# Attention in one layer of a hybrid backbone: transposing probabilities in pairs of key tiles, and masking only the outer blocks

## Chip, core and metric

The kernel runs on one core of a Trainium2 chip, in one launch. The metric is the device time of an execution in microseconds (us). The engines are TensorE (PE, with its weight loads listed apart as PEld), VectorE (DVE), ScalarE (ACT), GpSimd (POOL) and SyncE (SP), which issues the DMAs. TensorE writes only to PSUM, which has 8 banks of 512 fp32 values per partition; ScalarE and VectorE read the results from there.

## What is computed

One layer over 1024 latent tokens of width 1024, with a prefix of 256 context tokens. The part that the change touches is the two attention branches. Each has 8 query heads and 2 key/value heads of width 64. The local one sees the 256 context keys, the query block of 128 and its two neighbours, and a sink term in the softmax; the global one sees all 256 + 1024 keys.

```python
def window_attn(q, k, v, ck, cv, sink):            # local
    ...
    valid = (jnp.abs(kpos - qpos) <= WINDOW) & (kpos >= 0) & (kpos < S)   # WINDOW = BLOCK = 128
    s_loc = jnp.where(valid, s_loc, NEG_BIG)
    ...
    p = jax.nn.softmax(jnp.concatenate([s_ctx, s_loc, s_sink], axis=-1), axis=-1).astype(v.dtype)
    o = (jnp.einsum('bkgnqj,bjkd->bnqkgd', p[..., :n_ctx], cv)
         + jnp.einsum('bkgnqj,bnjkd->bnqkgd', p[..., n_ctx:n_ctx + 3 * BLOCK], vb))

def dense_attn(q, k, v, sink=None):                # global, in blocks of 128 queries
    s = jnp.einsum('bqkgd,bjkd->bkgqj', q.reshape(B_, Lq, KV, G, hd), k).astype(jnp.float32) * hd ** -0.5
    p = jax.nn.softmax(s, axis=-1)[..., :k.shape[1]].astype(v.dtype)
    return jnp.einsum('bkgqj,bjkd->bqkgd', p, v).reshape(B_, Lq, HQ * hd)
```

A key at most 128 positions away is valid. So in the middle block all 128 x 128 pairs are valid, in the block before it the keys from the query's own place on, and in the block after it the keys up to that place.

## The kernel before

**The whole.** The kernel goes through its stages one after the other: modulation and norms, projections of the context and of the latent tokens, the recurrence, token-major projections with rotary factors, local attention, global attention, the merge of the branches, and the gated MLP. Matrix products are done in fp32r, a rounded fp32 type: an operand is split into a rounded high part and the rest as a low part (on ScalarE and VectorE), and two or three products are summed.

**Order of the work.** The kernel is written for a framework that tracks the data, sets the semaphores and plans the order of each engine's instructions when it is built. The order of the program is the priority; `tc.high_priority(offset=...)` raises it. A planner then takes the first instruction that it holds to be ready, so that an engine's order can differ from the program's. On the chip each engine works in its planned order. `weave` (L1214) mixes generators in the program's order: it advances the one that has done the smallest share of its steps, by the number of steps given beside it.

**Attention.** `attention` (L1229) runs once for each branch (`br` 0 local, 1 global). Its loop has 16 iterations `it`: 8 query tiles `tt` of 128 queries by 2 key/value groups `g` of 4 heads. In each, three generators are woven: `scores(it + 1)`, `values(it)`, and gate products of another projection as filler (`gz`, L199 to L201). `qprep(it + 2)` loads and transposes queries ahead (`pq`, L1286). A query is held as high and low halves in one 128-row operand, so that a product with KH and one with KL gives the full score.

**Local scores** (`softmax_window`, L1374). For each head: two products of 256 columns with the context keys (L1387, L1388), two with the local keys (L1390, L1391), of 384 columns, or 256 at the first and last query tile, and one product of the identity with a table of 0 and -1e30 (`trir`, three blocks of 128 columns: before, middle, after) over all the local columns, which adds the mask (L1392). The middle block of the table is all zero. The maximum is taken on VectorE (L1395), the exponential on ScalarE (L1399), and GpSimd divides by the sum (L1409).

**Global scores** (`softmax_global`, L1415). There is no mask; the maximum is taken at L1427 and L1439, the exponentials at L1442 and L1443, and the division follows after the product with the values (`pr` L1316, `Rs` L1318).

**Values** (`values`, L1299). There are 10 key tiles in the global branch, 5 in the local one (4 at its two ends). For each key tile: four transposes of the heads' probabilities by the identity into one PSUM bank `pp` (L1321), a rounded copy `ph` on ScalarE (L1325), the rest `pl = pp - ph` on VectorE (L1326), and, two tiles later (`PV_LAG`), two products with the values, which sum in `po` (L1307, L1308). `pp`, `pq` and `pr` share two PSUM banks (tag "a"); `po` and the gate products share two others (tag "b"); the scores have the remaining four. `ph` and `pl` have three buffers each. Then `po` is put together on ScalarE and VectorE and stored (L1334 to L1344).

Of the kernel before, what the change touches and what calls it, by code (L numbers as in the profile page):

```python
# [9 lines left out]
F32 = mybir.dt.float32  # L10
F32R = mybir.dt.float32r
U32 = mybir.dt.uint32
AF = mybir.ActivationFunctionType
ALU = mybir.AluOpType
# [4 lines left out]
P = 128  # L19
# [41 lines left out]
PV_BUF = 3  # L61
PV_LAG = 2
V_PRIO = 15
# [1150 lines left out]
def weave(*gens):  # L1214

    gens = [[g, max(n, 1), 0] for g, n in gens if g is not None]
    while gens:
        gens.sort(key=lambda e: e[2] / e[1])
        e = gens[0]
        try:  # L1220
            next(e[0])
            e[2] += 1
            if e[2] > 4 * e[1]:
                raise RuntimeError("step count")
        except StopIteration:
            gens.remove(e)


def attention(tc, nc, ap_, br, ins, kv_d, q_d, y_d, mm2, bank, ident, identr, fill_gen, fill_steps):  # L1229
    V, A, G, T, SP = nc.vector, nc.scalar, nc.gpsimd, nc.tensor, nc.sync  # L1230

    def tl(shape, tag, nm, bufs=2, dt=F32):
        return ap_.tile(shape, dt, tag=tag, name=f"{tag}{br}_{nm}", bufs=bufs)

    NK = 10
    KH = tl([P, 2, NK * P], "KH", 0, 1, F32R)
    KL = tl([P, 2, NK * P], "KL", 0, 1, F32R)
    VHL = tl([P, NK, 2, 2, 64], "VHL", 0, 1, F32R)
    if br == 0:
        tri = tl([P, 3 * P], "tri", 0, 1, F32)  # L1240
        SP.dma_start(tri, ins["tri"])
        trir = tl([P, 3 * P], "trir", 0, 1, F32R)
        A.copy(trir, tri)
        snk = tl([P, 8], "snk", 0, 1)
        SP.dma_start(snk, ins["sink"].to_broadcast([P, 8]))
        nsnk = tl([P, 8], "nsnk", 0, 1)
        V.tensor_scalar(out=nsnk, in0=snk, scalar1=-1.0, scalar2=None, op0=ALU.mult)

    def prep(k0):
        kv = tl([P, 2, 256], "qf", f"kv{k0}")  # L1250
        SP.dma_start(kv, kv_d[k0:k0 + 2].rearrange("k p n -> p k n"))
        kx = kv[:, :, :128].rearrange("p k (g e) -> p k g e", g=2)
        vx = kv[:, :, 128:].rearrange("p k (g e) -> p k g e", g=2)
        vh, vl = VHL[:, k0:k0 + 2, :, 0], VHL[:, k0:k0 + 2, :, 1]
        A.copy(vh, vx)
        V.tensor_tensor(out=vl, in0=vx, in1=vh.bitcast(F32), op=ALU.subtract)
        for part, dst in ((0, KH), (1, KL)):
            if part == 0:
                kk = tl([P, 2, 2, 2, 64], "qs", f"kk{k0}{part}", dt=F32R)
                A.copy(kk[:, :, :, 0], kx)  # L1260
                A.copy(kk[:, :, :, 1], kx)
                kh = kk
            else:
                kk = tl([P, 2, 2, 2, 64], "qs", f"kk{k0}{part}", dt=F32R)
                for dup in range(2):
                    V.tensor_tensor(out=kk[:, :, :, dup], in0=kx, in1=kh[:, :, :, 0].bitcast(F32), op=ALU.subtract)
            pt = bank("a", f"kt{br}{k0}{part}", (P, 2, 2, P), F32R)
            for k in range(2):
                for g in range(2):
                    T.transpose(pt[:, g, k], kk[:, k, g].rearrange("p a b -> p (a b)"), identr)  # L1270
            A.copy(dst[:, :, k0 * P:(k0 + 2) * P].rearrange("p g (k c) -> p g k c", k=2), pt)

    QTs = {}

    def qprep(it):

        tt, g = divmod(it, 2)
        qf = tl([P, 4, 64], "qf", f"q{it}")
        SP.dma_start(qf, q_d[tt][:, g * 256:(g + 1) * 256])
        qs = tl([P, 4, 2, 64], "qs", f"q{it}", dt=F32R)  # L1280
        A.activation(qs[:, :, 0], qf, AF.Copy, scale=QSCALE)
        V.scalar_tensor_tensor(out=qs[:, :, 1], in0=qf, scalar=QSCALE, in1=qs[:, :, 0].bitcast(F32),
                               op0=ALU.mult, op1=ALU.subtract)
        pq = bank("a", f"pq{br}{it}", (P, 4, P), F32R)
        for h in range(4):
            T.transpose(pq[:, h], qs[:, h].rearrange("p a b -> p (a b)"), identr)  # L1286
        QT = tl([P, 4, P], "QT", it, 3, F32R)
        A.copy(QT, pq)
        QTs[it] = QT

    def scores(it):
        tt, g = divmod(it, 2)
        QT = QTs.pop(it)
        if br == 0:
            yield from softmax_window(nc, tl, mm2, tt, g, f"{it}_", QT, KH, KL, trir, identr, snk, nsnk, res)
        else:
            yield from softmax_global(nc, tl, mm2, g, f"{it}_", QT, KH, KL, res, rs)

    def values(it, PT, kts):  # L1299
        tt, g = divmod(it, 2)  # L1300
        Rs = None
        po = bank("b", f"po{br}{it}", (P, 4, P))
        prev = []

        def pv(n, kt, ph, pl):
            vv = VHL[:, kt, g].rearrange("p a b -> p (a b)")
            T.matmul(po, vv, ph, start=n == 0, stop=False)  # L1307
            T.matmul(po, vv, pl, start=False, stop=n == len(kts) - 1)  # L1308

        for n, kt in enumerate(kts):  # L1310
            if it in rs and n == 2:

                r = rs.pop(it)
                pr = bank("a", f"pr{br}{it}", (P, 2, P))
                for a in range(2):
                    T.matmul(pr[:, a], r[:, a * P:(a + 1) * P], ident, start=True, stop=True)  # L1316
                Rs = tl([P, 2, P], "ytmp", f"R{it}")
                A.copy(Rs, pr)  # L1318
            pp = bank("a", f"pp{br}{it}{kt}")
            for h in range(4):  # L1320
                T.transpose(pp[:, h], PT(h, n), ident)  # L1321
            ph = tl([P, 4, P], "ph", f"{it}{kt}", PV_BUF, F32R)
            pl = tl([P, 4, P], "pl", f"{it}{kt}", PV_BUF, F32R)
            with tc.high_priority(offset=V_PRIO):
                A.copy(ph, pp)  # L1325
                V.tensor_tensor(out=pl, in0=pp, in1=ph.bitcast(F32), op=ALU.subtract)  # L1326
            prev.append((n, kt, ph, pl))
            if len(prev) > PV_LAG:
                pv(*prev.pop(0))
            yield  # L1330
        for e in prev:
            pv(*e)

        yT = tl([P, 2, P], "yT", it)  # L1334
        pv_ = po.rearrange("p (a r) c -> p a r c", r=2)
        tmp = tl([P, 2, P], "ytmp", it)
        A.copy(tmp[0:64], pv_[64:128, :, 0])
        A.copy(tmp[64:128], pv_[0:64, :, 1])
        for r in range(2):
            sl = slice(r * 64, r * 64 + 64)  # L1340
            V.tensor_tensor(out=yT[sl], in0=pv_[sl, :, r], in1=tmp[sl], op=ALU.add)
        if Rs is not None:
            V.tensor_tensor(out=yT, in0=yT, in1=Rs, op=ALU.mult)
        SP.dma_start(y_d[br].rearrange("k p t -> p k t")[:, 2 * g:2 * g + 2, tt * P:(tt + 1) * P], yT)  # L1344
        yield

    n_it = 2 * LT
    res, rs = {}, {}
    def lead():
        for k0 in range(0, NK, 2):  # L1350
            prep(k0)
            yield
        qprep(0)
        qprep(1)
        yield
        yield from scores(0)

    weave((lead(), 10 + br), (some(fill_gen, FILL0), FILL0))
    fill_steps -= FILL0
    man = ExitStack()  # L1360
    if MAN[br]:
        man.enter_context(tc.manual_schedule(engines={mybir.EngineType.PE}))
    for it in range(n_it):
        PT, kts = res.pop(it)
        if it + 2 < n_it:
            qprep(it + 2)
        a, b = (min(fill_steps, int(fill_steps * i / (n_it - SKEW[br]))) for i in (it, it + 1))
        weave((scores(it + 1), S_LEN * (4 + br)) if it + 1 < n_it else (None, 0),
              (values(it, PT, kts), len(kts) + 1),
              (some(fill_gen, b - a), b - a))  # L1370
    man.close()


def softmax_window(nc, tl, mm2, tt, g, nm, QT, KH, KL, trir, identr, snk, nsnk, res):  # L1374
    V, A, G, T = nc.vector, nc.scalar, nc.gpsimd, nc.tensor
    lo, hi = max(tt - 1, 0), min(tt + 1, LT - 1)
    kts = [0, 1] + [2 + b for b in range(lo, hi + 1)]
    nk = len(kts) * P
    w = nk - 256
    m0 = (lo - (tt - 1)) * P  # L1380
    Ps = []
    st = tl([P, 8, 4], "st", nm)
    ng, sm, sk = st[:, 0], st[:, 1], st[:, 2]
    for h in range(4):

        sc = mm2(f"sa{nm}{h}").rearrange("p a b -> p (a b)")[:, 256:256 + nk]
        T.matmul(sc[:, :256], QT[:, h], KH[:, g, :256], start=True, stop=False)  # L1387
        T.matmul(sc[:, :256], QT[:, h], KL[:, g, :256], start=False, stop=True)  # L1388
        k = (2 + lo) * P
        T.matmul(sc[:, 256:], QT[:, h], KH[:, g, k:k + w], start=True, stop=False)  # L1390
        T.matmul(sc[:, 256:], QT[:, h], KL[:, g, k:k + w], start=False, stop=False)  # L1391
        T.matmul(sc[:, 256:], identr, trir[:, m0:m0 + w], start=False, stop=True)  # L1392
        n1 = ng[:, h:h + 1]
        hs = g * 4 + h
        V.tensor_reduce(out=n1, in_=sc, axis=AX.X, op=ALU.max, negate=True)  # L1395
# [5 lines left out]
        if h % NB == NB - 1:  # L1401
            b = slice(h - NB + 1, h + 1)
# [174 lines left out]
```

## Time and profile before

| what | value |
|---|---|
| median of 3 runs | 2129.76 us (2128.22 to 2130.08) |
| the profiled execution, its own time | 2129.82 us |
| its span in the trace | 2127.9 us |
| local attention, about | 700 to 885 us |
| global attention, about | 910 to 1220 us |
| transposes of probabilities (L1321) | 236 groups of four |
| rounded copies (L1325), mean | 236, 587 ns |
| subtractions (L1326), mean | 236, 687 ns |

The profile comes from one execution. Its page lists the busy time of each engine, the chain of waits that ended last, and groups of instructions by line and tile; `out<-in` names the tile written and those read. A matmul's bar in it reaches from its start to a modelled end, so that bars of consecutive matmuls overlap; starts are recorded. A busy TensorE is therefore not a TensorE without gaps. Other views of the trace list the waits of each engine, the busy time in a given stretch, and the instructions in order of time.

### The profile page before, as it was taken

To read this page: it belongs to the slowest core of one execution; us is meant where nothing else is said; L and a number is where in the kernel's file an instruction comes from. 1 tells how busy PE (TensorE), PEld (TensorE's weight loads), DVE (VectorE), ACT (ScalarE), POOL (GpSimd) and SP (SyncE) were. 2 spreads that over 40 slices of the span, in tenths; PEclk is the share of its full clock that TensorE was granted. 3 is DMA by queue.
4 is the path that set the end of the run, shared out by engine and by line. 5 is a ranking of instruction groups with operands and counts; after the bars stand their busy time and mean duration, and the time that the engine had idled before them with its cause. 6 is when DMAs were issued, how large, how long until landed. Compare 5 with 4: busy or idle time off the path is not lost.

```text
span 2127.9 us, 30555 instructions
## 1 busy us (share of the span) xinstructions
PE 2085.8 (98%) x11686; PEld 1743.1 (82%) x11686; DVE 1380.5 (65%) x2299; ACT 1001.2 (47%) x1761; POOL 288.1 (14%) x257
## 2 busy tenths in 40 slices
PE   7999999999999999999999999999999999999997
PEld 4888888888988888878888788888888888888887
DVE  4736756636665777678887746569777777664423
ACT  4333333311123777678888734346445544453222
POOL 0000000010021222100000000011333344100111
PEclk9999999999999999999999999999999999999999
DMA  9511111136543211211100354641222222285342
GB/s 359 207 44 36 46 50 41 46 113 214 186 137 123 78 59 41 80 55 35 35 28 28 115 200 142 194 156 55 99 79 89 80 80 88 81 287 201 109 126 86
DMA packets 95490, 229.28 MB, mean 108 GB/s; under 512 B 10736, under 2 KB 35824, under 8 KB 94320
## 3 DMA queue, kind: packets, MB, share of 16 engines
q1 hardware_dynamic: 95344, 227.33, 32.1%
q8 instruction: 92, 1.51, 0.3%
q14 instruction: 54, 0.44, 0.1%
HBM read 181.68 MB, written 45.61 MB: 107 GB/s over the span
## 4 chain that ended last, share of the span: by engine, by line
PE 69%; DVE 3%; ACT 2%; issue 1%; DMA 1%; POOL 1%; SPq 0%; DVEq 0%; ACTq 0%; POOLq 0%
PE pp L1321 4%; PE gz L199 3%; PE dn L929 3%; PE dn L928 3%; PE dn L930 3%; PE gz L200 3%; PE gz L201 3%; PE up L852 2%; PE up L853 2%; PE up L854 2%; PE po L1307 2%; PE po L1308 2%; PE br L200 2%; PE br L201 2%; PE br L199 2%; PE upd L853 2%
## 5 line engine op out<-in xcount | busy, mean ns | idle before, releaser
L175 ACT CAST wh<-wr 128x1024 fp32r<-128x1024 f32 (+1 forms) x139 | 145.1, 1044 | 398.7 <-PE dn L929 69.1
L176 DVE TENSOR_TENSOR wl<-wr,wh 128x1024 fp32r<-128x1024 f32 (+1 forms) x139 | 171.1, 1232 | 221.1 <-ACT wh L175 206.7
L1326 DVE TENSOR_TENSOR pl<-pp,ph 128x512 fp32r<-128x512 f32 x236 | 159.3, 687 | 29.2 <-ACT ph L1325 23.5
L199 PE MATMUL gz<-hh,wh 128*128 128x512 f32 x384 | 156.3, 408 | 3.1 <-ACT gs L523 3.1
L1325 ACT CAST ph<-pp 128x512 fp32r<-128x512 f32 x236 | 135.7, 587 | 37.4 <-PE pp L1321 35.3
L201 PE MATMUL gz<-hh,wl 128*128 128x512 f32 x384 | 152.3, 397 | 0.0
L200 PE MATMUL gz<-hl,wh 128*128 128x512 f32 x384 | 152.1, 396 | 0.0
L210 PE MATMUL tm<-wl,hh 128*128 128x256 f32 x384 | 108.9, 283 | 3.3 <-DVE wl L176 3.3
L209 PE MATMUL tm<-wh,hh 128*128 128x256 f32 x384 | 108.9, 284 | 0.9 <-ACT qo L615 0.9
L211 PE MATMUL tm<-wh,hl 128*128 128x256 f32 x384 | 108.6, 283 | 0.0
L1307 PE MATMUL po<-ph,VHL 128*128 128x512 f32 x236 | 106.1, 450 | 1.4 <-ACT ph L1325 1.0
L929 PE MATMUL dn<-ac,wh 128*128 128x512 f32 x256 | 99.7, 390 | 0.0
L930 PE MATMUL dn<-ac,wl 128*128 128x512 f32 x256 | 99.6, 389 | 0.0
L928 PE MATMUL dn<-ac,wh 128*128 128x512 f32 x256 | 99.6, 390 | 0.0
L1308 PE MATMUL po<-pl,VHL 128*128 128x512 f32 x236 | 97.1, 411 | 0.1
L199 PEld LDWEIGHTS gz<-hh,wh 128*128 128x128 f32 x384 | 72.7, 189 | 17.2 <-ACT gs L523 5.2
L201 PEld LDWEIGHTS gz<-hh,wl 128*128 128x128 f32 x384 | 72.5, 189 | 15.0
L200 PEld LDWEIGHTS gz<-hl,wh 128*128 128x128 f32 x384 | 72.8, 190 | 11.6
L210 PEld LDWEIGHTS tm<-wl,hh 128*128 128x128 f32 x384 | 73.7, 192 | 4.3 <-DVE wl L176 4.0
L1321 PE MATMUL pp<-ident,plat 128*128 128x128 f32 x512 | 76.6, 273 | 0.0
L1321 PEld LDWEIGHTS pp<-ident,plat 128*128 128x128 f32 x512 | 62.7, 140 | 16.9 <-DVE pl L1326 1.2
L199 PE MATMUL br<-yh,wh 128*128 128x512 f32 x192 | 74.3, 390 | 1.6 <-ACT yh L1468 1.6
(1420 smaller groups left out, 5898.7 us busy)
## 6 DMA issues: line engine op xcount, KB each, us to landing
wr<-in_w_cm SPq DMA_DIRECT2D x48, 512.0 KB, 3.7
wr<-in_w_up SPq DMA_DIRECT2D x44, 512.0 KB, 3.5
wr<-in_w_down SPq DMA_DIRECT2D x33, 512.0 KB, 3.5
wmr<-in_w_mod SPq DMA_DIRECT2D x32, 512.0 KB, 4.5
gate_d<-gs SPq DMA_DIRECT2D x48, 256.0 KB, 2.3
sgt<-gate_d SPq DMA_DIRECT2D x24, 512.0 KB, 3.4
act_d<-u SPq DMA_DIRECT2D x22, 512.0 KB, 2.6
st<-act_d SPq DMA_DIRECT2D x44, 256.0 KB, 4.5
```

Source lines behind the costliest of these rows:

```text
L175: A.copy(hi[:, :n], raw[:, :n])
L176: (lo_eng or V).tensor_tensor(out=lo[:, :n], in0=raw[:, :n], in1=hi[:, :n].bitcast(F32), op=ALU.subtract)
L199: T.matmul(psl, wh[:, k, c], hh[:, k0 + k, cols], start=s, stop=False)
L200: T.matmul(psl, wh[:, k, c], hl[:, k0 + k, cols], start=False, stop=False)
L201: T.matmul(psl, wl[:, k, c], hh[:, k0 + k, cols], start=False, stop=e)
L210: T.matmul(psl, hh[:, k, toks], wl[:, k % 4, :], start=False, stop=False)
L928: T.matmul(z, w[0][:, c], h[0], start=s, stop=False)
L929: T.matmul(z, w[0][:, c], h[1], start=False, stop=False)
L930: T.matmul(z, w[1][:, c], h[0], start=False, stop=e)
L1307: T.matmul(po, vv, ph, start=n == 0, stop=False)
L1321: T.transpose(pp[:, h], PT(h, n), ident)
L1326: V.tensor_tensor(out=pl, in0=pp, in1=ph.bitcast(F32), op=ALU.subtract)
```

## The change

**Values.** Key tiles are taken in pairs. The transposes of both tiles are issued first, into both banks; then, for each tile of the pair, the products of the oldest waiting tile if two are waiting, and the copy and the subtraction of this tile. With an odd number of tiles the last is alone. The place of `pr` stays ahead of the third tile. A step of the generator is a pair now, and the number of steps given to `weave` follows: 6 instead of 11 in the global branch, 4 or 3 instead of 6 or 5 in the local one.

**Mask.** The product with the mask is made for each outer block by itself (128 columns), not for the middle one, and it is issued between the two products with the local keys. A middle query tile has two such products for each head, the first and the last query tile one.

```diff
-        for n, kt in enumerate(kts):
-            if it in rs and n == 2:
+        def cast(n, kt, pp):
+            ph = tl([P, 4, P], "ph", f"{it}{kt}", PV_BUF, F32R)
+            pl = tl([P, 4, P], "pl", f"{it}{kt}", PV_BUF, F32R)
+            with tc.high_priority(offset=V_PRIO):
+                A.copy(ph, pp)
+                V.tensor_tensor(out=pl, in0=pp, in1=ph.bitcast(F32), op=ALU.subtract)
+            prev.append((n, kt, ph, pl))
+
+        for n0 in range(0, len(kts), 2):
+            if it in rs and n0 == 2:
...
-            pp = bank("a", f"pp{br}{it}{kt}")
-            for h in range(4):
-                T.transpose(pp[:, h], PT(h, n), ident)
-            ph = tl([P, 4, P], "ph", f"{it}{kt}", PV_BUF, F32R)
-            pl = tl([P, 4, P], "pl", f"{it}{kt}", PV_BUF, F32R)
-            with tc.high_priority(offset=V_PRIO):
-                A.copy(ph, pp)
-                V.tensor_tensor(out=pl, in0=pp, in1=ph.bitcast(F32), op=ALU.subtract)
-            prev.append((n, kt, ph, pl))
-            if len(prev) > PV_LAG:
-                pv(*prev.pop(0))
+            pps = []
+            for n in range(n0, min(n0 + 2, len(kts))):
+                pp = bank("a", f"pp{br}{it}{kts[n]}")
+                for h in range(4):
+                    T.transpose(pp[:, h], PT(h, n), ident)
+                pps.append((n, kts[n], pp))
+            for e in pps:
+                if len(prev) == 2:
+                    pv(*prev.pop(0))
+                cast(*e)
             yield
...
-              (values(it, PT, kts), len(kts) + 1),
+              (values(it, PT, kts), (len(kts) + 1) // 2 + 1),
...
-        T.matmul(sc[:, 256:], QT[:, h], KL[:, g, k:k + w], start=False, stop=False)
-        T.matmul(sc[:, 256:], identr, trir[:, m0:m0 + w], start=False, stop=True)
+        for b in range(lo, hi + 1):
+            if b != tt:
+                o = 256 + (b - lo) * P
+                T.matmul(sc[:, o:o + P], identr, trir[:, (b - tt + 1) * P:(b - tt + 2) * P], start=False, stop=False)
+        T.matmul(sc[:, 256:], QT[:, h], KL[:, g, k:k + w], start=False, stop=True)
```

More of the change, by code (lines that the diff above doesn't have):

```diff
@@ L1379, in softmax_window @@
     w = nk - 256
-    m0 = (lo - (tt - 1)) * P
     Ps = []
```

## The prediction, made before the change was run

> **What bounds the kernel now.** I read the page's totals first, then the busy time of the two attention stages by themselves, then TensorE's waits inside them, and last the timeline around the lines that change.
>
> ```profile
> span 2127.9 us, 30555 instructions
> PE 2085.8 (98%) x11686; PEld 1743.1 (82%) x11686; DVE 1380.5 (65%) x2299; ACT 1001.2 (47%) x1761; POOL 288.1 (14%) x257
> ```
>
> ```profile
> 700.00:885.00 185.00, 182.23 (x1086) 156.40 (x1085) 145.59 (x445) 135.64 (x345) 49.63 (x64) 1.00 0.17 51
> 910.00:1220.00 310.00, 303.92 (x1742) 247.66 (x1741) 246.24 (x406) 253.53 (x534) 6.43 (x16) 1.00 0.14 46
> ```
>
> The first pair of rows is the page's, the second the busy time by stretch: length, then TensorE, its weight loads, VectorE, ScalarE, GpSimd, and after them the granted clock. The stretch from 700 to 885 us is the local attention, 910 to 1220 us the global one; all of the edit lies in these 495 us. TensorE is busy for 98% of both at full clock. VectorE and ScalarE stand at 73 to 82%: not the bound, but with little room when work comes in bursts. So in these stages a microsecond of TensorE work more or less is nearly a microsecond of time, and beside it only TensorE's waits can give or take.
>
> Its waits show better on the weight loads than on the matmuls, since a matmul's bar includes the time in which it drains, and short gaps vanish under it. These are the rows, for 700 to 1220 us, of the operations that the pairing reorders (waited for, total, times, longest):
>
> ```profile
> PEld po L1307 <- ACT ph L1325: 6.0, 19, 1.0
> PEld pr L1316 <- issue: 5.4, 11, 1.2
> PEld pp L1321 <- ACT QT L1288: 3.6, 10, 0.5
> PEld pp L1321 <- DVE pl L1326: 1.4, 5, 0.4
> PEld pp L1321 <- issue: 1.2, 5, 0.4
> PEld pp L1321 <- POOL pw L1409: 1.1, 4, 0.3
> PEld po L1308 <- DVE pl L1326: 1.0, 4, 0.5
> PEld pp L1321 <- ACT ytmp_R L1318: 1.0, 4, 0.2
> ```
>
> Together 20.7 us: the most that another order of transposes and products could win. The wait that pairing might make worse, a transpose that waits for the subtraction to free its PSUM bank (pp <- pl), is 1.4 us today.
>
> **The mask, step by step.** Before, every head and query tile has one mask product (L1392); after, one product of 128 columns for each outer block.
>
> ```profile
> L1392 PEld LDWEIGHTS sa<-trir,identr x64: 187/188/192, 700.0 to 876.9; 128*128 128x128 f32 x64
> L1392 PE MATMUL sa<-trir,identr x64: 277/336/343, 700.1 to 877.1; 128*128 128x384 f32 x48, 128*128 128x256 f32 x16
> ```
>
> That is 48 products of 384 columns (query tiles 1 to 6) and 16 of 256 columns (tiles 0 and 7). After, the 48 become 96 and the 16 stay 16, all of 128 columns: 112 products, 48 more than now, for 14,336 columns instead of 22,528. Whether that is a gain hangs on what a product of 128 columns costs. A bar's length doesn't tell (it has the drain in it); the distance from one start to the next does. The timeline of TensorE in the local attention (start, length):
>
> ```profile
> 760.32 0.28 PE L1387 MATMUL sa<-KH,QT 128*128 128x256 f32 x1
> 760.43 0.28 PE L1388 MATMUL sa<-KL,QT 128*128 128x256 f32 x1
> 760.55 0.34 PE L1390 MATMUL sa<-KH,QT 128*128 128x384 f32 x1
> 760.73 0.34 PE L1391 MATMUL sa<-KL,QT 128*128 128x384 f32 x1
> 760.90 0.33 PE L1392 MATMUL sa<-trir,identr 128*128 128x384 f32 x1
> 761.07 0.39 PE L199 MATMUL gz<-hh,wh 128*128 128x512 f32 x1
> ...
> 761.77 0.60 PE L1321 MATMUL pp<-ident,pw 128*128 128x128 f32 x4
> 762.12 0.48 PE L1307 MATMUL po<-ph,VHL 128*128 128x512 f32 x1
> 762.44 0.39 PE L1308 MATMUL po<-pl,VHL 128*128 128x512 f32 x1
> 762.67 0.40 PE L199 MATMUL gz<-hh,wh 128*128 128x512 f32 x1
> ```
>
> From 760.55 to 760.73 to 760.90 to 761.07 a product of 384 columns costs 0.175 us; from 760.32 to 760.55 one of 256 costs 0.115 us, and the mask's 16 of that size are put at the same. The masks of before thus cost 48 x 0.175 + 16 x 0.115 = 10.2 us. No masking product of 128 columns exists in this trace. The nearest row is the last projection (L928 to L930), which has 128 columns, operands of the same rounded type, and a new weight load for each:
>
> ```profile
> 2110.62 0.28 PE L930 MATMUL dl<-ac,wl 128*128 128x128 f32 x1
> 2110.74 0.28 PE L928 MATMUL dl<-ac,wh 128*128 128x128 f32 x1
> 2110.85 0.28 PE L929 MATMUL dl<-ac,wh 128*128 128x128 f32 x1
> 2110.96 0.28 PE L930 MATMUL dl<-ac,wl 128*128 128x128 f32 x1
> ```
>
> Three distances make 0.34 us, 0.113 each: as much as 256 columns. So there seems to be a floor of some 0.11 us for a product with its own weight load, and the new masks have such a load each. 112 x 0.113 = 12.7 us, against 10.2: **2.5 us more**. Per head in the middle, two products at 0.226 replace one at 0.175, +0.051 us; at the edges the price is unchanged. The other end is a price by columns, a third of 0.175, or 0.058: 112 x 0.058 = 6.5 us, 3.7 us less than before. I take the floor, because the row that shows it is of the same kind in columns, type and loads; -3.7 stays as the other end. The Trainium skill speaks for this other end: "TensorE: Matmul & The Clock Gate", section "Back-to-back issue gap", gives N / 2.4 + 2.5 ns for a warm isolated matmul, about 56 ns at 128 columns, by which the masks would fall to an estimated 6.3 us. The projection's rows at the full clock are twice that, so the measurement decides.
>
> The mask moves ahead of the last QK product; the head's maximum (L1395) still waits for one last product, 0.05 us later than now. Other products on TensorE hide that, as its 98% shows; without that cover the 48 heads would add 2.4 us once more.
>
> **The pairing.** It adds and removes no instruction and no transfer: 944 transposes, 236 casts, 236 subtractions and 472 products remain, and every DMA keeps its place on SP's queue. What moves, in program order, is T(n) P(n-2) T(n+1) P(n-1) to T(n) T(n+1) P(n-2) P(n-1), with casts behind the products that are two tiles older. Does an alternation between transposes and products cost something that halving it would save? The first product after transposes has a bar of 0.48 us where the others have 0.39. But the starts say otherwise: from 761.77 to 762.44 four transposes and one product take 0.67 us, and 762.44 to 762.67 is 0.23 for a product alone, so 0.44, or 0.11 each, is left for the transposes. That is the same floor again; the long bar only begins early, under the last transpose. I count a gain of **0**. The misreading would be worth 118 alternations x 0.09 = 10.6 us, which I don't believe.
>
> What is late next? The second transposes of a pair need the bank that the second subtraction of the pair before frees. The global attention has 16 x 10 key tiles in 310 us, 1.94 us each or 3.88 for a pair. The planner there has already put two groups of transposes close together once, with everything that frees their banks:
>
> ```profile
> 1061.01 1.12 ACT L1442 ACTIVATE plat<-sbl,st__10486 128x1024 f32<-128x1024 f32 x1
> ...
> 1061.24 0.60 PE L1321 MATMUL pp<-ident,plat 128*128 128x128 f32 x4
> ...
> 1062.11 0.50 ACT L1443 ACTIVATE pc__10487<-pc__10487,st__10486 128x256 f32<-128x256 f32 x1
> 1062.14 0.60 PE L1321 MATMUL pp<-ident,plat 128*128 128x128 f32 x4
> ...
> 1062.61 1.06 ACT L1325 CAST ph<-pp 128x512 fp32r<-128x512 f32 x2
> ...
> 1063.21 1.29 DVE L1326 TENSOR_TENSOR pl<-pp,ph 128x512 fp32r<-128x512 f32 x2 [0.36 <-ACT ph L1325]
> ```
>
> Although ScalarE was held by an exponential, both banks were free at 1063.21 + 1.29 = 1064.50, 3.26 us after the first transpose. The next pair's second group comes on average 3.88 + 0.44 = 4.32 us after it: 1.06 us to spare. So the typical pair costs nothing, and that cover, not any gain, is what I count on; if ScalarE or VectorE come over 1.06 us later than here, the rest is a stall. For the waits listed above I take no net change, with 3 us either way.
>
> **The sum.** The profiled execution took 2129.82 us (span 2127.9 and 1.9 around it), 0.06 above the median of 2129.76, so nothing needs correcting. 2129.8 + 2.5 + 0 = **2132.3 us**, 0.12% more; about 0.2% (4.3 us) is what a measurement of this kernel can tell from no change. Own range of this case: 2128 to 2136.
>
> **Rivals.**
>
> *The banks become the bound (slower).* TensorE takes products in order, so a transpose that waits for a bank holds up its pair's products, the next scores and the gate products behind it. One subtraction (half of the 1.29 us, 0.65) is what the mate adds to the release. There are 80 full pairs in the global and 32 in the local attention; if one pair in eight waits that long, 14 x 0.65 = 9.1 us: 2129.8 + 2.5 + 9.1 = 2141.4. It decides from the third such pair on, where 4.3 is passed. For it: VectorE and ScalarE at 80%, and only two banks. Against it: the planner fills a transposer's wait with gate or score products where it foresees one, and today's pp <- pl is 1.4 us. The Trainium skill, same page, section "Part 2: What happens when you issue a matmul", says that only weight loads are pulled ahead and matmuls stay in program order; the wait rows, which sit on weight loads, do not contradict it. Chance 0.22.
>
> *The waits shrink (faster).* Products two tiles older now stand behind eight transposes instead of four, so their cast is surer to be done (6.0 and 1.0 us of waits), and the casts of one tile overlap the subtraction of the other. If half of the 20.7 us goes, 2129.8 + 2.5 - 10.3 = 2122.0. Against it: pr and QT, 9.0 us of the sum, wait for things that pairing doesn't touch. Chance 0.18.
>
> *The mask is paid by columns.* 2129.8 - 3.7 = 2126.1, within 0.2%. For it only proportion speaks; against it the projection's 0.113. Chance 0.08.
>
> *The pairing isn't executed*, because the planner pulls the groups apart again. Then only the mask is left, and the time is the forecast's; it is part of that case.
>
> **How the numbers follow.** Forecast 0.52, with 0.43 of it within 0.2%, 0.08 above (2134.1 and more) and 0.01 below; the column price 0.07 same and 0.01 faster. Faster: 0.18 + 0.01 + 0.01 = 0.20; same 0.50; slower: 0.22 + 0.08 = 0.30. For eight in ten, the range goes from 2123 (most of the shrinking waits) to 2140 (most of the bank case).
>
> **What would show it.** Right: 112 masking products whose starts lie 0.11 us apart, about 12.7 us of them; a product after transposes still with a 0.48 us bar, in half as many places; pp <- pl below some 4 us; the listed waits within 3 us of 20.7 in sum. Wrong: masking products 0.06 us apart (column price); pp <- pl or pp <- ph among the largest waits (bank case); po <- ph and pr fallen by half (the faster case); or a difference that lies outside the two attention stages, of which nothing above speaks.

## The result and the profile after

The changed kernel takes 2141.65 us (median of 4 runs, 2137.59 to 2142.64) against 2129.92 us: a ratio of 1.0057, 95% interval 1.0045 to 1.0069. It is 11.7 us slower, and the prediction's range (2123 to 2140) does not hold it. The profiled execution of after is the fastest of its four, 2137.59 us, so its trace shows 7.8 of the 11.7 us.

The totals of after's page:

```profile
span 2135.8 us, 30641 instructions
PE 2089.4 (98%) x11734; PEld 1747.6 (82%) x11734; DVE 1386.2 (65%) x2299; ACT 1000.9 (47%) x1761; POOL 290.3 (14%) x257
```

TensorE has the 48 products more that the change adds and is "98% busy" as before; this view shows nothing of what happened. Where the time went is told by the first starts of three lines, which mark the beginning of the local attention, of the global one, and of the merge. Before (the numbers behind the durations are the first and the last start):

```profile
L1387 PE MATMUL sa<-KH,QT x64: 274/281/384, 699.6 to 876.6; 128*128 128x256 f32 x64
...
L1425 PE MATMUL sbc__8873<-KH,QT x4: 278/280/282, 909.1 to 910.3; 128*128 128x256 f32 x4
...
L199 PE MATMUL br<-yh,wh x192: 389/389/498, 1204.6 to 1344.7; 128*128 128x512 f32 x192
```

After:

```profile
L1394 PE MATMUL sa<-KH,QT x64: 274/280/387, 696.8 to 887.4; 128*128 128x256 f32 x64
...
L1436 PE MATMUL sbc__8921<-KH,QT x4: 280/282/283, 920.1 to 921.3; 128*128 128x256 f32 x4
...
L199 PE MATMUL br<-yh,wh x192: 387/389/506, 1212.0 to 1352.1; 128*128 128x512 f32 x192
```

The local attention takes 223.3 us instead of 209.5, 13.8 more. The global one takes 291.9 instead of 295.5, 3.6 less. What lies ahead of them is 2.8 us shorter and what follows 0.5 us longer, though no line of it was changed; so a difference of some 3 us between two traces needn't come from the change.

The waits on TensorE's weight loads from 700 to 1220 us, after, with the same operations as in the prediction:

```profile
PEld pp L1332 <- POOL pw L1420: 12.5, 19, 1.1
PEld po L1307 <- ACT ph L1314: 4.7, 14, 1.2
PEld pr L1325 <- issue: 4.6, 14, 0.5
PEld po L1308 <- DVE pl L1315: 4.4, 10, 0.5
PEld pp L1332 <- DVE pl L1315: 3.1, 7, 1.2
PEld pp L1332 <- ACT QT L1288: 1.9, 5, 0.5
PEld pp L1332 <- issue: 1.7, 5, 0.4
...
PEld pp L1332 <- ACT ytmp_R L1327: 0.5, 2, 0.2
```

One row stands out: transposes that wait for `pw`, the probabilities which GpSimd has divided by their sum, rose from 1.1 to 12.5 us. Only the local branch has this step. The wait for PSUM banks (pp <- pl) rose from 1.4 to 3.1. The eight rows add up to 33.4 us, where the prediction's eight make 20.7.

The timeline shows how this wait arises. After, around the end of one local iteration, TensorE first:

```profile
762.02 0.33 PE L1402 MATMUL sa<-trir,identr 128*128 128x128 f32 x2
762.19 0.39 PE L1403 MATMUL sa<-KL,QT 128*128 128x384 f32 x1
762.42 0.39 PE L199 MATMUL gz<-hh,wh 128*128 128x512 f32 x1
```

```profile
765.32 0.34 PE L1397 MATMUL sa<-KH,QT 128*128 128x384 f32 x1
765.49 0.33 PE L1402 MATMUL sa<-trir,identr 128*128 128x128 f32 x2
765.66 0.39 PE L1403 MATMUL sa<-KL,QT 128*128 128x384 f32 x1
765.89 1.37 PE L1332 MATMUL pp<-ident,pw 128*128 128x128 f32 x8
767.02 0.48 PE L199 MATMUL gz<-hh,wh 128*128 128x512 f32 x1
```

then the last head's maximum, exponential and division on the three other engines:

```profile
762.98 0.82 DVE L1406 TENSOR_REDUCE st__6928<-sa 128x1 f32<-128x640 f32 x1
```

```profile
764.08 0.79 ACT L1410 ACTIVATE pw<-sa,st__6928 128x640 f32<-128x640 f32 x1 [1.22 <-DVE st__6928 L1408]
```

```profile
765.64 0.80 POOL L1420 TENSOR_SCALAR pw<-pw,st__6928 128x640 f32<-128x640 f32 x1 [0.78 <-DVE st__6928 L1418]
```

The product behind the last head's starts at 762.42; the head's division ends at 765.64 + 0.80 = 766.44, 4.0 us later. TensorE's other work until the next iteration's transposes lasts until 765.89, 3.5 us. So the fourth transpose, the last head's, waits: the eight transposes would take 8 x 0.109 = 0.87 us, and they take 1.13, from 765.89 to 767.02. In the same place before, the last head's products were done at 761.07 (its row is in the prediction) and the transposes came at

```profile
765.41 0.60 PE L1321 MATMUL pp<-ident,pw 128*128 128x128 f32 x4
```

4.3 us later: the last tile's transposes and two products with the values stood between, which after stand ahead of the last head. A busy share of 98% cannot show this; the 12.5 us, spread over 16 iterations, are waits of at most 1.1 us.

The mask's price can be read here as well. From 765.49 to 765.89 the two masks and the last product take 0.40 us, where the last product and the one mask took 2 x 0.175 = 0.35 us before: 0.05 more, as predicted. But the starts don't lie 0.11 us apart. In the 32 middle heads that a gate product follows, the medians are 0.060 us from the first mask to the second, 0.109 from the second to the last product, and 0.229 from that to the gate product, where a product of 384 columns had 0.175. The price shows in the sum alone; the first distance by itself looks like the price by columns.

### The profile page after: what moved, and what is told of

Same layout as the page of the kernel before. It is cut to its first block, busy times and chain, and to the rows that moved or that the text cites. A ratio compares the mean times of both kernels' runs of the same rounds, so it can differ in the third digit from the quotient of the medians.

```text
span 2135.8 us, 30641 instructions
## 1 busy us (share of the span) xinstructions
PE 2089.4 (98%) x11734; PEld 1747.6 (82%) x11734; DVE 1386.2 (65%) x2299; ACT 1000.9 (47%) x1761; POOL 290.3 (14%) x257
## 4 chain that ended last, share of the span: by engine, by line
PE 64%; DVE 5%; ACT 3%; issue 2%; DMA 2%; POOL 1%; SPq 0%; ACTq 0%; POOLq 0%; DVEq 0%
PE pp L1332 4%; PE dn L929 3%; PE dn L930 3%; PE dn L928 3%; PE up L852 2%; PE up L853 2%; PE up L854 2%; PE gz L199 2%; PE gz L201 2%; PE gz L200 2%; PE po L1307 2%; PE br L200 2%; PE br L199 2%; PE br L201 2%; PE po L1308 2%
## 5 line engine op out<-in xcount | busy, mean ns | idle before, releaser
L1307 PE MATMUL po<-ph,VHL 128*128 128x512 f32 x236 | 101.1, 429 | 1.5 <-ACT ph L1314 1.0
L733 ACT ACTIVATE u<-c,cw 128x1024 f32<-128x1024 f32 x38 | 47.3, 1246 | 61.7 <-DVE c L889 33.2
L200 PE MATMUL br<-yl,wh 128*128 128x512 f32 x192 | 75.0, 392 | 0.3 <-DVE yl L1480 0.3
```

The source lines that it names most:

```text
L200: T.matmul(psl, wh[:, k, c], hl[:, k0 + k, cols], start=False, stop=False)
```

## The experiments

The theory formed from this: **the steps**. `weave` advances the values of one iteration by pairs now, so the last head of the next iteration's scores enters the program after all transposes, and GpSimd's result comes late. Rivals: **the banks** (a pair waits for the subtraction of the pair before), and **the mask** beyond its price. Each run is compared with the kernel before on the same chip, where that had medians of 2125.7 to 2128.7 us; ratios carry 95% intervals, and 0.1% is 2.1 us. Beside the time stands at places the length of the local attention in the run's trace, from the first score product to the first of the global attention (209.5 us before, 223.3 after); it comes from one execution each.

### The two halves

`e1_mask`: the diff of L1390 to L1392 alone.

> The mask alone, with the values stage of before. All theories price the mask at +0.047 us in each of 48 middle heads, 2.3 us: 2132.2 us against 2129.9, from 2131 to 2134. If the earlier place of the mask (between the two products with the local keys) upsets the planned order, the time is 2135 or more and the transposes' wait for GpSimd (pp <- pw, 12.5 us after and 1.1 before) is above 6 us.

Ratio 1.0030 (1.0019 to 1.0041), 6.4 us, with 216.0 us of local attention. More than the price of the products.

`e2_pair`: the rest of the diff alone.

> The pairing alone, in both branches, with the mask of before. If the loss comes from the pairing, whether by its steps or by its banks, 2139.4 us (the 2141.65 of after without 2.3), from 2136 to 2141, and pp <- pw stays at 9 us or more. If mask and pairing only hurt together, 2131 or less.

Ratio 1.0022 (1.0014 to 1.0031), 4.7 us, with 213.8 us of local attention and pp <- pw at 7.4. The expected 9.5 missed because the mask has the larger half. The two add up to 11.1, near the whole. Their waits on the weight loads (690 to 1230 us), with the mask alone:

```profile
PEld po L1308 <- DVE pl L1326: 5.9, 15, 0.5
...
PEld pp L1321 <- POOL pw L1412: 4.4, 7, 0.8
PEld sa L1386 <- ACT pw L1402: 2.6, 7, 0.7
```

and with the pairing alone:

```profile
PEld pp L1332 <- POOL pw L1417: 7.4, 14, 0.9
...
PEld pp L1332 <- DVE pl L1315: 4.8, 15, 1.2
```

### Where the pairing loses

`e3_pair_global`: pairs in the global branch alone. The diff of its pairs is against the changed kernel; the mask is that of before.

```diff
-        for n0 in range(0, len(kts), 2):
+        W = 2 if br == 1 else 1
+        for n0 in range(0, len(kts), W):
...
-              (values(it, PT, kts), (len(kts) + 1) // 2 + 1),
+              (values(it, PT, kts), (len(kts) + 1) // 2 + 1 if br == 1 else len(kts) + 1),
```

> Pairing in the global branch alone, mask and local branch as before. Theory of the steps (the local branch loses, because the next iteration's last scores come too late for GpSimd): the global stage is 3.6 us shorter as in the profile after, so 2126.3 us, from 2124.5 to 2129. Theory of the banks (each pair waits for the subtraction of the pair before): the 80 global pairs pay most of it, 2134 or more, and pp <- pl is above 6 us.

Ratio 0.9998 (0.9990 to 1.0007): no loss, which is against the banks, and no gain that can be told from zero; pp <- pl is 4.0 us. The local attention, unchanged here, takes 208.7 us. The 3.6 us that after's profile seemed to win in the global stage are not in the time.

`e4_steps`: no pairs, only the coarser steps.

```diff
-            yield
+            if n % 2 or n == len(kts) - 1:
+                yield
...
-              (values(it, PT, kts), len(kts) + 1),
+              (values(it, PT, kts), (len(kts) + 1) // 2 + 1),
```

> No pairing and the mask of before: transposes and products alternate by single tiles as before, but a step of the generator covers two tiles, and weave is given the smaller number of steps. Theory of the steps: the last head's scores are issued late again, so pp <- pw is 8 us or more and the time 2135 to 2141 us. Theory of the banks: nothing waits that did not wait before, 2129.9 us, within 2 us.

Ratio 1.0019 (1.0011 to 1.0027), as much as the pairing alone though below the 5 us and more that the theory asked for; the local attention takes 213.5 us, and the wait is there although transposes and products alternate by single tiles:

```profile
PEld pp L1321 <- POOL pw L1410: 8.5, 14, 1.0
```

`e13_pair_tile_steps` is the counterpart: pairs, the mask of before, a step for each tile and the old number of steps.

```diff
                 pps.append((n, kts[n], pp))
+                if n == n0 and n0 + 1 < len(kts):
+                    yield
...
-              (values(it, PT, kts), (len(kts) + 1) // 2 + 1),
+              (values(it, PT, kts), len(kts) + 1),
```

> Pairing with the mask of before, but the generator gives way after each tile and weave has the old number of steps. If the pairing's 4.7 us come from the coarser steps alone, the time is that of before within 1.5 us and pp <- pw is about 1 us; if some of it belongs to products that wait for both tiles, +2 to +3 us; if all of it, +4.7.

Ratio 1.0007 (0.9997 to 1.0017), 1.5 us, with 210.7 us of local attention and pp <- pw back at its value of before:

```profile
PEld pp L1332 <- POOL pw L1419: 1.1, 4, 0.3
```

Together the two runs show that the coarser steps carry most of the pairing's loss; what is left for the pairs themselves can't be told from zero.

`e8_pair_early` and `e5_early` keep the coarse steps and move the scores ahead.

```diff
-        weave((scores(it + 1), S_LEN * (4 + br)) if it + 1 < n_it else (None, 0),
+        weave((scores(it + 1), S_LEN * 5 if br else 10) if it + 1 < n_it else (None, 0),
```

> Pairing alone as in the run with pairing and the mask of before (4.7 us slower than before), and weave is told that the local scores have 10 steps instead of 5.4, so that the last head's scores enter the program's order earlier against the coarser values steps. Theory of the steps: pp <- pw falls from 7.4 to 2 us or less, and the time comes back to that of before, from -2 to +2 us. Theory of the pairs themselves (eight transposes in a row need a bank or an operand too early, in whatever order): still +4 us or more.

Ratio 1.0019 (1.0010 to 1.0028): the wait for GpSimd goes as expected, and the time stays. The rows of 690 to 930 us show what took its place:

```profile
PEld sa L1395 <- ACT pw L1407: 5.6, 16, 0.5
PEld gz L199 <- ACT gs L523: 4.0, 10, 0.8
PEld po L1308 <- DVE pl L1315: 3.4, 13, 0.5
...
PEld pp L1332 <- POOL pw L1417: 1.5, 5, 0.5
```

There is PSUM space for the scores of two heads. Where a head now follows closely on the one before, as at 755.26 us with one other product between, it waits until the exponential of the head two before it has read that space, and starts 0.14 us after its end. So removing the wait for GpSimd alone doesn't bring the time back. With coarse steps, the heads either come late or crowd: that the steps cost the time is shown, that they do it through this one wait is not.

> The whole change, with the local scores earlier in the same way (10 steps instead of 5.4). Theory of the steps: the pairing's 4.7 us go and the mask's 6.4 us stay, +5 to +8 us against before, pp <- pw below 6 us. If the mask's products and the late scores wait for the same thing (GpSimd's chain after the last head), both go: +2.3 us for the mask's products alone, from +1 to +4. If order has nothing to do with it: +10 or more.

With the mask of the change: 1.0039 (1.0025 to 1.0052), 8.3 us; sa <- pw is 9.2 us, pp <- pw 1.4. Its median is below that of the whole change, but the intervals overlap, and neither half is gone.

`e7_tile_steps`: the whole change with a step for each tile.

> The whole change, but the generator gives way after the first tile of a pair as well, and weave is given the old number of steps. Theory of the steps: as for the whole change with earlier scores, +5 to +8 us. Theory of the pairs: +10 us or more, since the products still come after both tiles.

Ratio 1.0041 (1.0028 to 1.0054), 8.7 us, between what the two theories said; pp <- pw is 1.1 us, and po <- pl 5.1, as with the mask alone.

### Where the mask loses

From the start of a middle head's first product to the start of the gate product behind it, the traces give 0.764 us before and 0.812 with the mask alone (medians): 48 x 0.048 = 2.3 us. That leaves 4 of the 6.4.

`e9_mask_place`: the old mask, between the two products.

```diff
-        T.matmul(sc[:, 256:], QT[:, h], KL[:, g, k:k + w], start=False, stop=False)
-        T.matmul(sc[:, 256:], identr, trir[:, m0:m0 + w], start=False, stop=True)
+        T.matmul(sc[:, 256:], identr, trir[:, m0:m0 + w], start=False, stop=False)
+        T.matmul(sc[:, 256:], QT[:, h], KL[:, g, k:k + w], start=False, stop=True)
```

> Neither pairs nor blocks: the one masking product of before over all local columns, moved between the two products with the local keys. If the mask's loss beyond its 2.3 us (6.4 measured with the mask alone) comes from the place, +4 us here, with po <- pl and pp <- pw grown as there; if it comes from the number and size of the products, no change, within 1 us.

Ratio 0.9995 (0.9986 to 1.0004), with 208.5 us of local attention. Not the place.

`e10_mask_end`: the blocks, behind the last product.

> Masking products of 128 columns on the outer blocks, as in the change, but behind the last product with the local keys, where the one mask of before stands; values as before. If the loss of the mask alone (6.4 us, of which 2.3 are the products' own price) hangs on the blocks, +5 to +8 us again; if it takes the blocks and the place together, +2.3 us, from +1 to +4.

Ratio 1.0021 (1.0013 to 1.0030), 4.5 us, just below what was expected, with 216.1 us of local attention; from 690 to 930 us po <- pl is 5.5 and pp <- pw 3.7 us, where the mask alone has 5.3 and 4.4. It hangs on the blocks.

`e11_mask_256`: two products of 256 columns.

```diff
-        T.matmul(sc[:, 256:], identr, trir[:, m0:m0 + w], start=False, stop=True)
+        for o in range(0, w - 128, 128):
+            T.matmul(sc[:, 256 + o:512 + o], identr, trir[:, m0 + o:m0 + o + 256], start=False, stop=o + 256 == w)
```

> The mask as two products of 256 columns in the middle query tiles (both cover the middle block, where the table is zero), one of 256 at the edges; place and values as before. TensorE pays 2 x 0.118 instead of 0.175 us in 48 heads, +2.9 us, a little more than with blocks of 128. If the rest of the mask's loss comes because TensorE has a product more in every head, +6 us or more; if it comes because products of 128 columns are planned otherwise than they run, only +2.9 us, from +2 to +4.

Ratio 1.0012 (1.0004 to 1.0021), 2.6 us: about the price, 48 x 0.061 = 2.9 us, though TensorE pays no less than with the blocks; a middle head takes 0.825 us. On the same chip the blocks at the same place cost 3.3 us more. In the trace the local attention takes 213.8 us, 4.3 more than before, so that some 1.5 us beyond the price are not excluded. The waits of 690 to 930 us keep the shape of before:

```profile
PEld po L1307 <- ACT ph L1325: 3.6, 11, 1.0
PEld pq L1286 <- DVE qs_q L1282: 2.5, 4, 0.9
...
PEld pp L1321 <- POOL pw L1410: 1.1, 4, 0.3
```

`e12_mask_one`: one block of 128 for each head; it leaves out the mask of the block after the query's own in the middle tiles.

```diff
-        T.matmul(sc[:, 256:], QT[:, h], KL[:, g, k:k + w], start=False, stop=False)
-        T.matmul(sc[:, 256:], identr, trir[:, m0:m0 + w], start=False, stop=True)
+        b = lo if lo < tt else hi
+        o = 256 + (b - lo) * P
+        T.matmul(sc[:, o:o + P], identr, trir[:, (b - tt + 1) * P:(b - tt + 2) * P], start=False, stop=False)
+        T.matmul(sc[:, 256:], QT[:, h], KL[:, g, k:k + w], start=False, stop=True)
```

> One masking product of 128 columns for each head, in the place of the change; values as before. It leaves out the mask of the block after the query's own in the middle tiles. 64 products at 0.112 us are 7.2 us against 10.3, 3.1 us less on TensorE. If the loss follows TensorE's time, this is 3 to 5 us faster than before; if a product of 128 columns upsets the planned order whatever it costs, -3.1 + 4.1 = +1 us, from 0 to +3.

Ratio 1.0008 (0.9999 to 1.0016), with 210.3 us of local attention. A middle head falls to 0.703 us, so TensorE does save its 3 us, and the kernel is not faster. The saving reappears as waits:

```profile
PEld po L1307 <- ACT ph L1325: 5.1, 11, 1.0
PEld gz L199 <- ACT gs L523: 1.8, 6, 0.8
PEld sa L1387 <- ACT pw L1401: 1.6, 3, 0.8
```

against 1.8, 1.0 and 0.5 us before, in the same stretch. This fits two readings: products of 128 columns are planned otherwise than they run, or the other engines' chains hold this stage. Four runs with TensorE's order in the local branch taken from the program were to tell them apart:

```diff
-MAN = (False, False)
+MAN = (True, False)
```

> Before, but TensorE's order in the local attention is that of the program, written by weave, instead of the planner's. It is the base for the next three. The planner hides waits, so this may be slower than before by up to 10 us; all theories agree on it.

Ratio 1.0056 (1.0043 to 1.0070), 2138.76 us: a fixed order is 12 us slower, with 220.9 us of local attention and a long wait for GpSimd:

```profile
PEld pp L1321 <- POOL pw L1409: 9.6, 6, 2.0
```

Part of it is the clock. In the traces of all four runs with the fixed order TensorE is granted half the clock for 3.4 us at about 708 us, inside the local attention, and in this one a second time at 820.6 us; the trace of before has no such stretch there. Each can cost at most 1.7 us.

> The mask of the change (blocks of 128 columns between the two products), TensorE's order in the local attention that of the program, so that the products keep their places among the others. If the 4 us beyond the products' price come from the planner's other order, this is 2.3 us above the base with the fixed order, from 1 to 4. If the chip itself pays them around a product of 128 columns, 6 us or more above it.

1.0073 (1.0060 to 1.0086), 2141.87 us: 3.1 us above the fixed base in the medians, near the price of 2.3. But intervals of 0.13% each way can't part 2.3 from 6. The traces lean to the price: 222.4 us of local attention against 220.9, 1.5 more, or at most 3.2 if the base's second half-clock stretch cost its full 1.7.

> One masking product of 128 columns for each head and the fixed order; it leaves out the mask of the block after the query's own in the middle tiles. TensorE pays 3.1 us less than the base with the fixed order. If TensorE's time is returned in full, -3.1 us, from -4.5 to -1.5; if the local stage is held by the other engines' chains, so that less work on TensorE is only more waiting, 0, from -1 to +1.

1.0060 (1.0045 to 1.0076), 2140.96 us: 3.1 us less on TensorE, and the median is not below the base's. But the six runs go from 2134.5 to 2142.7 us, and the intervals leave room for the 3.1 us; this run decides nothing by itself. The wait of the scores for the exponential (sa <- pw) grows from 1.9 to 4.9 us.

> Pairing alone with the mask of before and the fixed order in the local attention. Theory of the steps: the program's order itself issues the last head too late, so against the base with the fixed order the loss is as large as with the planner or larger, +4 us or more, with pp <- pw among the largest waits. If the planner made the loss, 0, within 1.5 us.

1.0023 (1.0013 to 1.0033), 2131.10 us: against both theories, pairing with a fixed order is 7.7 us faster than the fixed base, of which the base's second half-clock stretch is at most 1.7. Its wait for GpSimd is about half of the base's:

```profile
PEld pp L1332 <- POOL pw L1417: 5.0, 11, 0.9
```

So pairs with coarse steps are not bad in themselves; they are worse than the order which the planner makes of the fine steps, and better than the fine steps in the program's order.

The traces of the mask's runs also show what the planner did. The table takes the instructions of the local attention in the order of their starts, by the tiles that they write and read, and counts the places where they differ from before: of TensorE's 1152 products and transposes without the masks, and of VectorE's 466 instructions. It counts the tiles, of 76, whose subtraction `pl` starts more than 0.4 us after the copy `ph` has ended, and gives the wait po <- pl from 690 to 930 us.

| mask | TensorE, other places | VectorE, other places | late subtractions | po <- pl, us |
|---|---|---|---|---|
| before | | | 14 | 0.4 |
| one of 384 columns, between the products | 0 | 0 | 14 | 0.4 |
| two of 256 columns | 19 | 94 | 15 | 0.2 |
| one block for each head | 58 | 115 | 17 | 0.6 |
| blocks, at the end | 97 | 181 | 29 | 5.5 |
| blocks, in the place of the change | 105 | 176 | 29 | 5.3 |

So the planner does order the work of both engines otherwise for the blocks, and VectorE's subtractions come late with it. The runs with a fixed order left VectorE's order to the planner: with the blocks 30 subtractions are late there, without them 20, and po <- pl is 5.1 us against 1.3. They test TensorE's share of the planner's order, then, and not VectorE's.

## Why the prediction was wrong

**The price of the mask's products was right.** 0.051 us a head were predicted and 0.048 measured, 2.3 us instead of 2.5. In sum the floor of 0.11 us for a product of 128 columns holds; by columns a head would have taken about 0.705 us and not 0.812. But the sign named for it, starts 0.11 us apart, did not come: they are 0.060 and 0.109, with the rest on the product behind, and by the prediction's own sign 0.06 would have meant the price by columns. The 56 ns of the Trainium skill's formula for an isolated matmul ("TensorE: Matmul & The Clock Gate", section "Back-to-back issue gap") are near that first distance, but half of the price.

**No cost for alternating was right.** The global branch, with 80 pairs, gained nothing (0.9998), where the misreading's 0.09 us for each pair would have been 7.2 us; so the long bar behind transposes was no cost to save.

**"For the waits listed above I take no net change, with 3 us either way" is the step that failed.** The pairing alone costs 4.7 us, where the sum has 0. The eight listed waits went from 20.7 to 33.4 us in the profile. Most of it is one row that the prediction quoted at 1.1 us and passed over, pp <- POOL pw. The working costed the bank's release as "what is late next" and never the other operand of the transposes: the probabilities of the last head. The line of the diff that changes the number of steps for `weave` was not costed at all, and that line alone, with its coarser yields, gives as much loss as the pairing (1.0019 and 1.0022).

**The mask's term in the sum failed too, although its price was right.** The sum has 2.5 us for the mask; the mask alone costs 6.4 us (4.0 to 8.7). The prediction took the price of the products for the whole effect and weighed beside it only a maximum that comes 0.05 us later; what the blocks do to the order and the waits of the other engines had no term.

**"A microsecond of TensorE work more or less is nearly a microsecond of time" failed as well.** Some 3 us less work on TensorE returned nothing in the planner's order (1.0008, 0.9999 to 1.0016). More work of 2.9 us cost 2.6 in one form and, for 2.3 us of price, 6.4 and 4.5 in another. That chains through the other engines hold the local stage as closely as TensorE does would fit this; it was argued from the waits and not shown.

**The rival of the banks** named a time close to the result, 2141.4, but by luck: its mechanism isn't the cause, since pp <- pl stayed at 3.1 us, and the global branch did not lose.

**What stays open** is why blocks of 128 columns cost some 4 us beyond their price while products of 256 columns cost little more than theirs. The place is excluded, the number of products too. That the planner orders TensorE's and VectorE's work otherwise is shown by the traces, and the late subtractions with it; that this costs the 4 us is argued and not shown. A run with the orders of both engines fixed would tell. Nor does it explain the run with one block for each head, where few subtractions are late and the 3 us don't come back.

## What to carry to other kernels

When a change makes steps coarser in a woven schedule, follow every operand of the moved instructions back to its last producer and compare that chain's length with the work left between, even if its wait is small today. A near-full bar on one engine doesn't prove that this engine's work converts into time; a run that takes some of its work away tells. And a small matmul should be priced by starts over a whole row, up to the second product behind it, and not by one distance: here two products of 128 columns cost more than one of 384, though the first of them is followed after 0.060 us. The price is not the whole effect, either: the planner may order the other engines' work anew.

## What the runs showed of the hardware

Products of this rounded type with 128 columns start 0.113 us apart in the row of the last projection, those with 256 columns 0.115 to 0.120 us in the scores, each with its own weight load of 0.188 us in the profile, while one of 384 columns costs 0.175. Behind a product of 384 columns, two of 128 start 0.060 and 0.109 us ahead of what follows them, and the product of 384 columns behind them takes 0.229 us: the sum is as if each of 128 cost 0.11. The kernel before, unchanged, ran between 2123 and 2134 us on the chips used, so that a change of 0.12% was only just told from none with 11 runs against 35.
